# A hybrid decoder step on one core: the sample block's top-k laid over all 128 partitions

## The chip, the cores and the metric

The kernel runs on one core of a Trainium2 chip. The metric is the device time of one execution in microseconds (us); three executions of the kernel before took 1877.14, 1884.6 and 1884.9 us, median 1884.6.

## What is computed

One layer for 576 tokens: 512 of a prompt and 64 of a sample (8 sequences of 8 new tokens with a cache of 2048 positions). Attention with 12 heads over three dilated windows and a short convolution are joined by an output projection; then comes a channel mixer (PEER) that picks, for every token and each of 8 heads, 16 of 16384 single-neuron experts. That mixer is where the change lies:

```python
q = (xc @ wq).reshape(-1, 8, 2, 128)                 # 16 column blocks: head, half
s = einsum('nhpc,hpkc->nhpk', q, sub_keys)           # 128 scores per head and half
sv, si = top_k(s, 16)                                # first top-k: 16 of 128
cand = sv[:, :, 0, :, None] + sv[:, :, 1, None, :]   # pairs; ids likewise from si
top, pos = top_k(cand, 16)                           # second top-k: 16 experts per head
g = softmax(top)
act = gelu(einsum('nd,nhkd->nhk', x, u[eid]))
out = einsum('nhk,nhkd->nd', g * act, v[eid])
```

## The kernel before

The 576 tokens lie in five blocks: 0 to 3 are the prompt's, 128 tokens each; block 4 is the sample, 64 tokens. Tokens lie on partitions. All float32 products are made as three products of a high and a low part: `split` (L102) lets ScalarE copy the high part (L103) and VectorE subtract it (L104).

Instructions are written in program order, and a scheduler then sets the order on each engine; it may pull an instruction of a later stage forward to where it expects the engine to be free. Within an engine the order is fixed after that. Each engine, and each DMA queue (SP's here), takes its instructions one after the other.

The stages, with the names that the trace shows:

- Projections and attention (to about 480 us), with block 0 taken through the mixer's top-k early.
- `group(GB, ...)` for blocks 1 to 4: output projection (to about 560 us), then the loop over 16 column blocks of `wq` (L690), one for each head and half. Each step loads and splits the weights (`wraw`, `whi`, `wlo`), makes the queries of all 448 tokens (`mm`), copies them (`qc`, L698), multiplies them by the sub-keys (L703), copies the scores (`scs`, L705 for the three full blocks and L707 for the sample's 64 rows) and calls `topk1` for each block.
- `topk1` (L490) is five VectorE instructions on one head and half: eight largest (L495), replaced by a very small number (L496, writes `tkw`), the next eight (L497), and the places of both (L498, L499). Results go to `sv` and `si`.
- `topk2` (L501) takes a block's 8 heads: candidate pairs and their ids (`cand`, `cid`, L515), five instructions per head on 50 candidates (L523 to L527), the softmax (`gt` or `gatg`), and then the chosen ids by comparing, multiplying and summing over wide int16 tiles (`oh`, L547, L549, L554).
- The three prompt blocks 1 to 3 don't gather experts: all 16384 are computed (dense), and the chosen gates are placed in a table G. `gbuild` (L812) makes that table from `topk2`'s result, with one-hot tiles on VectorE (`oj`, L844; `oi`, L848), a scaled copy on ScalarE (`oi`, L852), products (`pG`) and a copy out (`stg`, L860) that is stored to DRAM (`Gd`).
- `ustep` (L773) is one of 128 steps of the dense mixer's first half: load 128 experts (`ur`), split (`uh`, `ul`), 24 products of 384 columns (`pu`), gelu (`a`, L782), and for the first 68 steps a store (`Ad`). These 68 are written between the pieces of `gbuild`.
- Then a loop over 128 steps of the second half (L935): the other 60 usteps come with it, each step loads `vr`, splits it, multiplies the gelu outputs by the table (`w`, L898) and makes 18 products of 512 columns (`y`, L909 to L913).
- Blocks 0 and 4 gather their experts instead: POOL fetches a row of `u` or `v` for each of 128 partitions (`row`, L469), VectorE takes the dot product (`jk`, L477) or adds it in (`accg`, L487). 128 rows of each table for block 0, 64 for the sample, which has 128 choices per token but lies on 64 partitions: its second half of choices is moved to partitions 64 to 127 (L572 to L574) and both halves are added at the end. This work is pushed in small units between the other stages (`pump`).

Of the kernel before, what the change touches and what calls it, by code (L numbers as in the profile page):

```python
# [19 lines left out]
P = 128  # L20
# [47 lines left out]
def body(tc, I, O):  # L68
# [421 lines left out]
    def topk1(st, cc, b, n, src):  # L490
        hd_, p_ = divmod(cc, 2)
# [9 lines left out]
    def topk2(st, b, n, ef, gat):  # L501
        sv, si = st[b]
        sf = tk.tile([P, 8, 2, 16], F32, name="sf")
        nc.vector.tensor_copy(sf[:n], si[:n])
        nc.vector.tensor_scalar(sf[:n, :, 0, :], sf[:n, :, 0, :], 128.0, None, op0=OP.mult)
        cand = tk.tile([P, 8, NCAND], F32, name="cand")
        cid = tk.tile([P, NCAND, 8], I16, name="cid")
        for src, dst in ((sv, cand), (sf, cid.rearrange("p w h -> p h w"))):
            o = 0
            for (a0, a1_, nb_) in PAIRS:  # L510
                na = a1_ - a0
                out = dst[:n, :, o:o + na * nb_].rearrange("p h (a b) -> p h a b", b=nb_)
                i0 = src[:n, :, 0, a0:a1_].unsqueeze(3).to_broadcast([n, 8, na, nb_])
                i1 = src[:n, :, 1, 0:nb_].unsqueeze(2).to_broadcast([n, 8, na, nb_])
# [3 lines left out]
        tv = tk.tile([P, 8, 16], F32, name="tv")  # L518
        tp = tk.tile([P, 8, 16], U32, name="tp")
        wc = tk.tile([P, NCAND], F32, name="wc", bufs=2)  # L520
        for hd_ in range(8):
            src = cand[:n, hd_, :]
            nc.vector.max(tv[:n, hd_, 0:8], src)  # L523
            nc.vector.match_replace(wc[:n], tv[:n, hd_, 0:8], src, -3.0e38)
            nc.vector.max(tv[:n, hd_, 8:16], wc[:n])
            nc.vector.max_index(tp[:n, hd_, 0:8], tv[:n, hd_, 0:8], src)
            nc.vector.max_index(tp[:n, hd_, 8:16], tv[:n, hd_, 8:16], wc[:n])  # L527
            if hd_ % 2:
                yield 1.2
        tf = tk.tile([P, 16, 8], I16, name="tf")  # L530
        nc.vector.tensor_copy(tf[:n], tp[:n].rearrange("p h k -> p k h"))
        te = tk.tile([P, 8, 16], F32, name="te")
        nc.vector.tensor_tensor(te[:n], tv[:n], tv[:n, :, 0:1].to_broadcast([n, 8, 16]), op=OP.subtract)
        nc.scalar.activation(te[:n], te[:n], AF.Exp)
        dn = tk.tile([P, 8], F32, name="dn")
        nc.vector.tensor_reduce(dn[:n], te[:n], axis=mybir.AxisListType.X, op=OP.add)
        nc.vector.reciprocal(dn[:n], dn[:n])
        nc.vector.tensor_tensor(gat[:n].rearrange("p (h k) -> p h k", h=8), te[:n],
                                dn[:n].unsqueeze(2).to_broadcast([n, 8, 16]), op=OP.mult)
        yield 1.0  # L540
        efv = ef[:n].rearrange("p (h k) -> p h k", h=8)
        for k0 in (0, 8):
            w = FIRST[k0 + 7] + 1
            oh = tk.tile([P, NCAND, 8, 8], I16, name="oh")
            ohf = oh.rearrange("p w k h -> p w (k h)")
            sel = tf[:n, k0:k0 + 8, :].rearrange("p k h -> p (k h)").unsqueeze(1).to_broadcast([n, w, 64])
            nc.vector.tensor_tensor(ohf[:n, :w], iotaw[:n, :w], sel, op=OP.is_equal)  # L547
            yield 1.7
            nc.vector.tensor_tensor(oh[:n, :w], oh[:n, :w], cid[:n, :w].unsqueeze(2).to_broadcast([n, w, 8, 8]),  # L549
                                    op=OP.mult)  # L550
            yield 1.7
            while w > 1:
                m = w - w // 2
                nc.vector.tensor_tensor(ohf[:n, :w - m], ohf[:n, :w - m], ohf[:n, m:w], op=OP.add)  # L554
                w = m
            nc.vector.tensor_copy(efv[:, :, k0:k0 + 8], oh[:n, 0].rearrange("p k h -> p h k"))
            yield 2.0

    def topk_gather(st, b, n, k):
        ef = tk.tile([P, SLOTS], F32, name="ef", bufs=2)  # L560
        if n == P:
            yield from topk2(st, b, n, ef, gatg[k])
            nc.vector.tensor_copy(idxg[k], ef)
            return
        gt = tk.tile([P, SLOTS], F32, name="gt", bufs=2)
        ei = tk.tile([P, SLOTS], I32, name="ei")
        yield from topk2(st, b, n, ef, gt)
        hs = SLOTS // 2
        nc.vector.tensor_copy(ei[:n], ef[:n])
        nc.vector.tensor_copy(idxg[k][:n, :hs], ef[:n, :hs])  # L570
        nc.vector.tensor_copy(gatg[k][:n, :hs], gt[:n, :hs])
        nc.sync.dma_start(idxg[k][n:2 * n, :hs], ei[:n, hs:])  # L572
        nc.sync.dma_start(gatg[k][n:2 * n, :hs], gt[:n, hs:])
        nc.sync.dma_start(x2g[k][n:2 * n, :], x2g[k][:n, :])  # L574

    def group(grp, st, chp, clp, mm, psc, x2dst, lname, pre2=None):
# [113 lines left out]
        for cc in range(16):  # L690
# [9 lines left out]
            sc = gp.tile([P, 4, P], F32, name="scs", bufs=2)  # L700
# [3 lines left out]
            full = [bi for bi, b in enumerate(grp) if BLKS[b][1] == P]  # L704
            nc.scalar.activation(sc[:, :len(full), :], p2[:, :len(full), :], AF.Copy)  # L705
# [329 lines left out]
```

## Time and profile before

| | |
|---|---|
| three executions | 1877.14, 1884.6, 1884.9 us |
| profiled execution, first to last instruction | 1882.2 us (no other time of it is given) |
| PE busy | 1738.2 us, 92% |
| VectorE (DVE) busy | 1430.9 us, 76%, 3064 instructions |
| ScalarE (ACT) busy | 881.6 us, 47% |
| POOL busy | 579.0 us, 31% |
| DMA | 533.75 MB, mean 284 GB/s |
| mean granted TensorE clock | 0.955 of full |

Busy shares are means over stages with different limits; the rows further down take the stages apart. Matmuls overlap each other, so a stretch in which PE is busy throughout may still hold fewer matmuls than another of the same length.

### The profile page before, as it was taken

Reading aid. Unit: us, or ns where it says so; the run is one execution under the profiler, and the core shown is the slowest. Engines: PE = TensorE matmul, PEld = TensorE weight load, DVE = VectorE, ACT = ScalarE, POOL = GpSimd, SP = SyncE. Lnnn points to the kernel's source line nnn. Section 1 sums busy time; section 2 is a strip of 40 time slices with the busy share of each in tenths; the row PEclk is TensorE's granted clock in tenths of the full one; section 3 lists DMA queues with packets and bytes.
Section 4 is the critical chain, followed back from the end, with each engine's and each line's share of the span. In section 5 each row is a group of like instructions: output and inputs, shape, how many; then the busy total and the mean of one; then the engine's idle time right before and its main releaser. Section 6 shows DMA issues by size and latency. Waiting matters only on the chain. (4 is left out here: it accounts for less than half of the span.)

```text
span 1882.2 us, 29066 instructions
## 1 busy us (share of the span) xinstructions
PE 1738.2 (92%) x10391; PEld 1467.3 (78%) x10391; DVE 1430.9 (76%) x3064; ACT 881.6 (47%) x1615; POOL 579.0 (31%) x483
## 2 busy tenths in 40 slices
PE   7999899997679999988988999999999999999997
PEld 5778655654558998987978889999999997777776
DVE  5433235766888999998788578888888778888888
ACT  4222366645323333479999933333333333333334
POOL 1010201014554214311212234544444444333330
PEclk9999979978788999999999999999999999999999
DMA  4257569858898448867777699999999999999996
GB/s 143 100 181 288 208 245 337 316 185 291 302 320 302 154 143 312 277 216 267 266 261 250 253 365 330 353 335 348 331 336 341 320 361 334 363 344 367 340 349 210
DMA packets 199077, 533.75 MB, mean 284 GB/s; under 512 B 17586, under 2 KB 82660, under 8 KB 197268
## 3 DMA queue, kind: packets, MB, share of 16 engines
q1 hardware_dynamic: 133364, 294.22, 44.0%
q0 software_dynamic: 65568, 237.69, 35.5%
q8 instruction: 81, 1.33, 0.3%
q14 instruction: 64, 0.52, 0.1%
HBM read 485.65 MB, written 45.63 MB: 282 GB/s over the span
## 5 line engine op out<-in xcount | busy, mean ns | idle before, releaser
L469 POOL DMA_INDIRECT row<-in_u,idxg x192 | 257.9, 1343 | 457.6 <-DVE avg L477 231.4
L469 POOL DMA_INDIRECT row<-in_v,idxg x192 | 264.5, 1377 | 421.6 <-DVE accg L487 345.3
L107 PE MATMUL pu<-x2h,uh 128*128 128x384 f32 x1024 | 350.9, 343 | 21.4 <-ACT a L782 11.1
L109 PE MATMUL pu<-x2h,ul 128*128 128x384 f32 x1024 | 352.0, 344 | 7.5 <-DVE ul L104 7.3
L108 PE MATMUL pu<-x2l,uh 128*128 128x384 f32 x1024 | 348.8, 341 | 0.0
L103 ACT ACTIVATE vh<-vr 128x1024 fp32r<-128x1024 f32 x128 | 135.8, 1061 | 290.4 <-PE y L913 251.4
L477 DVE CUSTOM_DVE_ANT_0 jk<-row,x2g 128x1024 bf16<-128x1024 f32 x192 | 233.8, 1218 | 28.0 <-DMA row<-in_u,idxg 26.8
L487 DVE SCALAR_TENSOR_TENSOR accg<-row,avg,accg 128x1024 f32<-128x1024 f32 x190 | 243.2, 1280 | 7.7 <-DMA row<-in_v,idxg 6.7
L909 PE MATMUL y<-vh,wh 128*128 128x512 f32 x768 | 224.7, 395 | 15.5 <-ACT wh L103 15.5
L911 PE MATMUL y<-vl,wh 128*128 128x512 f32 x768 | 234.2, 393 | 0.0
L107 PEld LDWEIGHTS pu<-x2h,uh 128*128 128x128 f32 x1024 | 196.5, 192 | 27.1 <-ACT a L782 12.2
L104 DVE TENSOR_TENSOR vl<-vr,vh 128x1024 fp32r<-128x1024 f32 x128 | 156.6, 1224 | 77.9 <-ACT vh L103 74.9
L913 PE MATMUL y<-vh,wl 128*128 128x512 f32 x768 | 215.6, 390 | 0.0
L109 PEld LDWEIGHTS pu<-x2h,ul 128*128 128x128 f32 x1024 | 196.4, 192 | 12.4 <-DVE ul L104 10.1
L103 ACT ACTIVATE uh<-ur 128x1024 fp32r<-128x1024 f32 x128 | 136.0, 1064 | 145.1 <-PE pu L108 74.1
L108 PEld LDWEIGHTS pu<-x2l,uh 128*128 128x128 f32 x1024 | 196.3, 192 | 1.7
L104 DVE TENSOR_TENSOR ul<-ur,uh 128x1024 fp32r<-128x1024 f32 x128 | 156.2, 1220 | 35.9 <-ACT uh L103 34.2
L909 PEld LDWEIGHTS y<-vh,wh 128*128 128x128 f32 x768 | 143.9, 189 | 46.5 <-ACT wh L103 19.5
L911 PEld LDWEIGHTS y<-vl,wh 128*128 128x128 f32 x768 | 145.1, 189 | 30.4
L913 PEld LDWEIGHTS y<-vh,wl 128*128 128x128 f32 x768 | 144.0, 188 | 30.1
L104 DVE TENSOR_TENSOR wlo<-wraw,whi 128x1024 fp32r<-128x1024 f32 (+1 forms) x96 | 91.0, 952 | 67.5 <-ACT whi L103 67.1
L103 ACT ACTIVATE whi<-wraw 128x1024 fp32r<-128x1024 f32 (+1 forms) x96 | 79.8, 840 | 124.3 <-PE mm L109 53.7
(281 smaller groups left out, 2936.4 us busy)
## 6 DMA issues: line engine op xcount, KB each, us to landing
ur<-in_ut SPq DMA_DIRECT2D x128, 512.0 KB
vr<-in_v SPq DMA_DIRECT2D x128, 512.0 KB
kt<-in_ck SPq DMA_DIRECT2D x60, 512.0 KB
vt<-in_cv POOLq DMA_DIRECT2D x60, 512.0 KB
Gd<-stg SPq DMA_DIRECT2D x12, 2048.0 KB
gt<-Gd SPq DMA_DIRECT2D x32, 768.0 KB
wraw<-in_w_in SPq DMA_DIRECT2D x24, 512.0 KB
Ad<-a SPq DMA_DIRECT2D x62, 192.0 KB
```

The lines of the kernel that those rows point to most:

```text
L103: nc.scalar.activation(hi, src, AF.Copy)
L104: nc.vector.tensor_tensor(lo, src, hi.bitcast(F32), op=OP.subtract)
L107: nc.tensor.matmul(out, ah, bh, start=first, stop=False)
L108: nc.tensor.matmul(out, ah, bl, start=False, stop=False)
L109: nc.tensor.matmul(out, al, bh, start=False, stop=last)
L469: nc.gpsimd.indirect_dma_start(out=r, out_offset=None, in_=I[src], in_offset=bass.IndirectOffsetOnAxis(ap=idx[:, s:s + 1], axis=0))
L477: nc.vector.tensor_tensor_reduce(jk, r, x2, 1.0, 0.0, OP.mult, OP.add, av[:, s:s + 1]))
L487: nc.vector.scalar_tensor_tensor(acc, r, av[:, s:s + 1], acc, op0=OP.mult, op1=OP.add))
L909: nc.tensor.matmul(accs[b][k], wh[:, sl], vh[:, k * 512:k * 512 + 512], start=first, stop=False)
L911: nc.tensor.matmul(accs[b][k], wh[:, sl], vl[:, k * 512:k * 512 + 512], start=False, stop=False)
L913: nc.tensor.matmul(accs[b][k], wl[:, sl], vh[:, k * 512:k * 512 + 512], start=False, stop=last)
```

## The change

The sample's scores for heads 4 to 7 are written to partitions 64 to 127, those of heads 0 to 3 stay on partitions 0 to 63. The score product of the 64 sample tokens goes to rows 0 or 64 of its bank, and the copy to a tile `sc4` keeps them there. One `topk1` on 128 partitions then serves two heads, so the column blocks of `wq` are taken in the order 0, 8, 1, 9, ... and the sample's `topk1` is called at every second one. `topk2` for the sample runs with 4 heads on 128 partitions, and gates and ids come out where the gather wants them. The copies and the two DMAs that moved them there are gone; the DMA that copies the sample's normed rows (`x2g`) to partitions 64 to 127 stays.

The diff, cut to its core (of `topk2` a few lines stand for all: `n` and 8 become `P` and `H`):

```diff
     def topk1(st, cc, b, n, src):
-        hd_, p_ = divmod(cc, 2)
+        hd_, p_ = divmod(cc % 8 if b == 4 else cc, 2)
...
-    def topk2(st, b, n, ef, gat):
+    def topk2(st, b, H, ef, gat):
         sv, si = st[b]
+        K = 8 * H
-        cand = tk.tile([P, 8, NCAND], F32, name="cand")
+        cand = tk.tile([P, 8, NCAND], F32, name="cand")[:, :H]
...
-        for hd_ in range(8):
-            src = cand[:n, hd_, :]
+        for hd_ in range(H):
+            src = cand[:, hd_, :]
...
-            nc.vector.tensor_tensor(ohf[:n, :w], iotaw[:n, :w], sel, op=OP.is_equal)
+            nc.vector.tensor_tensor(ohf[:, :w], iotaw[:, :w, :K], sel, op=OP.is_equal)
...
-        gt = tk.tile([P, SLOTS], F32, name="gt", bufs=2)
-        ei = tk.tile([P, SLOTS], I32, name="ei")
-        yield from topk2(st, b, n, ef, gt)
-        hs = SLOTS // 2
-        nc.vector.tensor_copy(ei[:n], ef[:n])
-        nc.vector.tensor_copy(idxg[k][:n, :hs], ef[:n, :hs])
-        nc.vector.tensor_copy(gatg[k][:n, :hs], gt[:n, :hs])
-        nc.sync.dma_start(idxg[k][n:2 * n, :hs], ei[:n, hs:])
-        nc.sync.dma_start(gatg[k][n:2 * n, :hs], gt[:n, hs:])
-        nc.sync.dma_start(x2g[k][n:2 * n, :], x2g[k][:n, :])
+        if H < 8:
+            nc.sync.dma_start(x2g[k][64:128, :], x2g[k][:64, :])
+        yield from topk2(st, b, H, ef, gatg[k][:, :16 * H])
+        nc.vector.tensor_copy(idxg[k][:, :16 * H], ef)
...
-        for cc in range(16):
+        for cc in [c for lo in range(8) for c in (lo, lo + 8)]:
...
+            up_ = cc // 8 * 64
             for bi, b in enumerate(grp):
                 t0, n = BLKS[b]
-                nc.tensor.matmul(p2[:n, bi, :], qc[:, t0 - g0:t0 - g0 + n], skT[:, cc, :], start=True, stop=True)
+                r0 = up_ if n < P else 0
+                nc.tensor.matmul(p2[r0:r0 + n, bi, :], qc[:, t0 - g0:t0 - g0 + n], skT[:, cc, :], start=True, stop=True)
...
+            if not up_:
+                sc4 = gp.tile([P, P], F32, name="sc4", bufs=2)
+            nc.scalar.activation(sc4[up_:up_ + 64, :], p2[up_:up_ + 64, nb - 1, :], AF.Copy)
+            for bi, b in enumerate(grp[:-1]):
+                topk1(st, cc, b, P, sc[:, bi, :])
+            if up_:
+                topk1(st, cc, 4, P, sc4)
...
-    drain(topk_gather(st, 4, 64, 1))
+    drain(topk_gather(st, 4, 4, 1))
```

What this does to the order, at three places. The first is VectorE in the `wq` loop; `sv_5199` and `si_5200` are the sample's results, the other numbers are those of blocks 1 to 3. Before, one step's turn of the four blocks:

```order
L495 MAX sv_5195<-scs 128x8
L495 MAX sv_5197<-scs 128x8
L496 MATCH_REPLACE tkw<-sv_5195,scs 128x128
L495 MAX sv_5199<-scs 64x8
...
L498 MAX_INDEX si_5200<-sv_5199,scs 64x8
...
L499 MAX_INDEX si_5200<-sv_5199,tkw 64x8
```

Now the sample reads its own tile (`sc_6294`) and stands there in every second step only:

```order
L495 MAX sv_5195<-scs 128x8
L495 MAX sv_5197<-scs 128x8
L496 MATCH_REPLACE tkw<-sv_5193,scs 128x128
L495 MAX sv_5199<-sc_6294 128x8
...
L498 MAX_INDEX si_5200<-sv_5199,sc_6294 128x8
L497 MAX sv_5195<-tkw 128x8
L499 MAX_INDEX si_5194<-sv_5193,tkw 128x8
```

In all, VectorE issues 62 rows fewer: 40 of `topk1`, 20 of the heads in `topk2`, 2 copies. The second place is VectorE where the table G is done (last `oj`) and the second half's loop begins (first `w`). Before:

```order
L844 TENSOR_TENSOR oj<-iotaj,JT 128x1024
L104 TENSOR_TENSOR ul<-ur,uh 128x1024 x6
L104 TENSOR_TENSOR vl<-vr,vh 128x1024
L898 TENSOR_TENSOR w<-a,gt 128x384 x2
L104 TENSOR_TENSOR wl<-w,wh 128x384
```

Now (lines here are those of the changed kernel: `oj` is L838, `w` L892):

```order
L838 TENSOR_TENSOR oj<-iotaj,JT 128x1024
L104 TENSOR_TENSOR ul<-ur,uh 128x1024
L487 SCALAR_TENSOR_TENSOR accg_2404<-row,avg_2407,accg_2404 128x1024
...
L104 TENSOR_TENSOR ul<-ur,uh 128x1024
L104 TENSOR_TENSOR vl<-vr,vh 128x1024 x2
L892 TENSOR_TENSOR w<-a,gt 128x384
L104 TENSOR_TENSOR wl<-w,wh 128x384
```

Six `ul` stand between the two in both, but they are other steps: counted from the start, before has 29 `ul` ahead of the first `oj`, 68 ahead of the last and 74 ahead of the first `w`; now it is 26, 63 and 69. Ahead of the 20th `w` it is 89 and 90. From the 60th `w` on both have the same counts of every kind (128 `ul`, 176 `jk`, 128 `accg`). The third place is SP's DMA queue near the end of the table; before:

```order
L863 DMA Gd<-stg 128x4096
L767 DMA ur<-in_ut 128x1024 x2
L572 DMA idxg_5203<-ei 64x64
L767 DMA ur<-in_ut 128x1024 x2
L863 DMA Gd<-stg 128x4096
```

Now:

```order
L761 DMA ur<-in_ut 128x1024 x2
L857 DMA Gd<-stg 128x4096
L761 DMA ur<-in_ut 128x1024 x2
L761 DMA vr<-in_v 128x1024
L885 DMA gt<-Gd 128x12x128
```

The two DMAs of `idxg` and `gatg` no longer stand among the loads of `ur`; the one of `x2g` stands at the same place as before, ahead of the `wq` loop.

## Rows read from the trace of the kernel before

**Rows 1.** The page's busy shares, then PE's 40 slices of the span.

```profile
PE 1738.2 (92%) x10391; PEld 1467.3 (78%) x10391; DVE 1430.9 (76%) x3064; ACT 881.6 (47%) x1615; POOL 579.0 (31%) x483
PE   7999899997679999988988999999999999999997
```

**Rows 2.** Windows by stage: stretch, length, busy time by engine, clock, DMA.

```profile
587.00:801.00 214.00, 207.58 (x1138) 196.10 (x1138) 207.02 (x848) 74.12 (x117) 67.98 (x48) 0.99 0.68 226
801.00:1068.00 267.00, 232.33 (x1668) 219.70 (x1667) 226.46 (x483) 252.29 (x552) 58.22 (x34) 0.94 0.72 254
811.00:1072.00 261.00, 229.60 (x1672) 217.46 (x1673) 218.13 (x459) 252.52 (x558) 56.74 (x33) 0.94 0.73 259
1300.00:1569.00 269.00, 269.00 (x1357) 244.06 (x1355) 219.46 (x270) 93.72 (x127) 123.43 (x96) 1.00 0.95 337
```

**Rows 3.** Windows of 20 us: PE at full pace, then three holes.

```profile
740.00:760.00 20.00, 20.00 (x117) 20.00 (x116) 19.37 (x67) 10.19 (x13) 5.63 (x5) 1.00 0.86 291
720.00:740.00 20.00, 15.48 (x79) 14.84 (x78) 18.21 (x73) 5.60 (x7) 11.33 (x7) 0.91 0.85 280
880.00:900.00 20.00, 14.06 (x97) 13.25 (x96) 18.73 (x55) 18.59 (x40) 5.31 (x3) 0.83 0.66 232
980.00:1000.00 20.00, 15.29 (x96) 14.08 (x95) 14.33 (x24) 19.94 (x42) 1.28 (x1) 0.74 0.62 231
```

**Rows 4.** Waits from 697 to 800 us: who for whom, us in total, times, longest.

```profile
ACT uh L103 <- DMA ur<-in_ut: 30.3, 10, 4.9
ACT uh L103 <- PE pu L108: 24.4, 9, 7.4
PEld pu L109 <- DVE ul L104: 8.0, 7, 3.5
```

**Rows 5.** Waits from 800 to 1043 us.

```profile
DVE oi L848 <- ACT oi L852: 14.3, 9, 3.1
PE pu L107 <- ACT a L782: 11.1, 5, 2.8
ACT uh L103 <- PE pu L108: 9.2, 3, 5.9
ACT stg L860 <- PE pG L858: 4.3, 3, 1.9
```

**Rows 6.** Timeline of VectorE: start, us, instruction; one turn of four blocks.

```profile
658.37 0.27 DVE L495 MAX8 sv<-scs 128x8 f32<-128x128 f32 x1
...
663.04 1.20 DVE L477 CUSTOM_DVE_ANT_0 jk<-row,x2g 128x1024 bf16<-128x1024 f32 x1
```

**Rows 7.** Groups by shape: line, engine, operation, count | busy us, mean ns | idle before.

```profile
L498 DVE FIND_INDEX8 si<-sv,scs 128x8 uint32<-128x128 f32 x48 | 13.1, 280 | 0.0
L498 DVE FIND_INDEX8 si<-sv,scs 64x8 uint32<-64x128 f32 x16 | 4.5, 280 | 0.0
L547 DVE TENSOR_TENSOR oh<-iotaw,tf 64x3200 int16<-64x3200 int16 x1 | 1.8, 1819 | 0.0
L547 DVE TENSOR_TENSOR oh<-iotaw,tf 64x2624 int16<-64x2624 int16 x1 | 1.5, 1508 | 0.0
L554 DVE TENSOR_TENSOR oh<-oh 64x1600 int16<-64x1600 int16 x1 | 1.0, 978 | 0.0
L554 DVE TENSOR_TENSOR oh<-oh 64x64 int16<-64x64 int16 x3 | 0.5, 182 | 0.0
L103 ACT ACTIVATE uh<-ur 128x1024 fp32r<-128x1024 f32 x128 | 136.0, 1064 | 145.1 <-PE pu L108 74.1 <-DMA ur<-in_ut 45.7 <-issue 16.2
L782 ACT ACTIVATE a<-pu 128x384 f32<-128x384 f32 x128 | 61.7, 482 | 19.8 <-PE pu L109 18.9 <-ACT a L782 0.9
```

**Rows 8.** SP's own waits from 800 to 1100 us.

```profile
SPq L767 <- DVE idxg L570: 3.8, 1, 3.8
SPq L767 <- DVE gt L538: 3.0, 1, 3.0
```

**Rows 9.** Line 898: count, ns shortest/median/longest, first and last start.

```profile
L898 DVE TENSOR_TENSOR w<-a,gt x66: 545/552/559, 1093.7 to 1857.3; 128x384 f32<-128x384 f32 x66
```

More of the change, by code (lines that the diff above doesn't have):

```diff
@@ L511, in topk2 @@
                 na = a1_ - a0
[L512 to L514 removed]
+                out = dst[:, :, o:o + na * nb_].rearrange("p h (a b) -> p h a b", b=nb_)
+                i0 = src[:, :, 0, a0:a1_].unsqueeze(3).to_broadcast([P, H, na, nb_])
+                i1 = src[:, :, 1, 0:nb_].unsqueeze(2).to_broadcast([P, H, na, nb_])
                 nc.vector.tensor_tensor(out, i0, i1, op=OP.add)
@@ L517, in topk2 @@
             yield 1.2
-        tv = tk.tile([P, 8, 16], F32, name="tv")
-        tp = tk.tile([P, 8, 16], U32, name="tp")
+        tv = tk.tile([P, 8, 16], F32, name="tv")[:, :H]
+        tp = tk.tile([P, 8, 16], U32, name="tp")[:, :H]
         wc = tk.tile([P, NCAND], F32, name="wc", bufs=2)
-        for hd_ in range(8):
-            src = cand[:n, hd_, :]
[L523 to L527, printed above, removed]
+        for hd_ in range(H):
+            src = cand[:, hd_, :]
+            nc.vector.max(tv[:, hd_, 0:8], src)
+            nc.vector.match_replace(wc, tv[:, hd_, 0:8], src, -3.0e38)
+            nc.vector.max(tv[:, hd_, 8:16], wc)
+            nc.vector.max_index(tp[:, hd_, 0:8], tv[:, hd_, 0:8], src)
+            nc.vector.max_index(tp[:, hd_, 8:16], tv[:, hd_, 8:16], wc)
@@ L528, in topk2 @@
             if hd_ % 2:
                 yield 1.2
[L530 to L536, printed above, removed]
@@ L537, in topk2 @@
-        nc.vector.reciprocal(dn[:n], dn[:n])
-        nc.vector.tensor_tensor(gat[:n].rearrange("p (h k) -> p h k", h=8), te[:n],
-                                dn[:n].unsqueeze(2).to_broadcast([n, 8, 16]), op=OP.mult)
+        tf = tk.tile([P, 16 * 8], I16, name="tf")[:, :16 * H].rearrange("p (k h) -> p k h", h=H)
+        nc.vector.tensor_copy(tf, tp.rearrange("p h k -> p k h"))
+        te = tk.tile([P, 8, 16], F32, name="te")[:, :H]
+        nc.vector.tensor_tensor(te, tv, tv[:, :, 0:1].to_broadcast([P, H, 16]), op=OP.subtract)
@@ L540, in topk2 @@
+        nc.scalar.activation(te, te, AF.Exp)
+        dn = tk.tile([P, 8], F32, name="dn")[:, :H]
+        nc.vector.tensor_reduce(dn, te, axis=mybir.AxisListType.X, op=OP.add)
+        nc.vector.reciprocal(dn, dn)
+        nc.vector.tensor_tensor(gat.rearrange("p (h k) -> p h k", h=H), te,
+                                dn.unsqueeze(2).to_broadcast([P, H, 16]), op=OP.mult)
         yield 1.0
-        efv = ef[:n].rearrange("p (h k) -> p h k", h=8)
+        efv = ef.rearrange("p (h k) -> p h k", h=H)
@@ L542, in topk2 @@
         for k0 in (0, 8):
             w = FIRST[k0 + 7] + 1
-            oh = tk.tile([P, NCAND, 8, 8], I16, name="oh")
-            ohf = oh.rearrange("p w k h -> p w (k h)")
-            sel = tf[:n, k0:k0 + 8, :].rearrange("p k h -> p (k h)").unsqueeze(1).to_broadcast([n, w, 64])
-            nc.vector.tensor_tensor(ohf[:n, :w], iotaw[:n, :w], sel, op=OP.is_equal)
+            ohf = tk.tile([P, NCAND * 64], I16, name="oh")[:, :NCAND * K].rearrange("p (w c) -> p w c", c=K)
+            oh = ohf.rearrange("p w (k h) -> p w k h", h=H)
@@ L714, in mkst @@
     def mkst(pl, grp):
-        return {b: (pl.tile([P, 8, 2, 16], F32, name=f"sv{b}"), pl.tile([P, 8, 2, 16], U32, name=f"si{b}"))
-                for b in grp}
+        return {b: tuple(pl.tile([P, 4 if b == 4 else 8, 2, 16], dt, name=f"{nm}{b}")
+                         for nm, dt in (("sv", F32), ("si", U32))) for b in grp}
     st0 = mkst(keep2, GA)
@@ L814, in gbuild @@
         gt = tk.tile([P, SLOTS], F32, name="gt", bufs=2)
-        yield from topk2(st, b, P, ef, gt)
+        yield from topk2(st, b, 8, ef, gt)
         ei = tk.tile([P, SLOTS], I32, name="ei")
```

35 lines of the change are left out of this document (13 added, 22 removed).

## The prediction, on record before the changed kernel ran

> **What bounds the kernel now.** First the page: PE is busy 92% of the span, VectorE 76%, and of its 40 slices most from the 14th on show a full PE [rows 1]. A share of the whole span says little here, so I cut the part that the change touches into stretches. Stretch A, 587 to 801 us, holds the `wq` loop with its top-k and then the second top-k of the first dense block. In it VectorE is busy 207.0 of 214.0 us and PE 207.6 [rows 2]. Stretch B, 801 to 1068 us, builds the table G; there ScalarE is busy 252.3 of 267 us, VectorE 226.5, PE 232.3 [rows 2]. Behind it the second half's loop keeps PE busy without a gap, 269.00 of 269 us from 1300 to 1569 [rows 2].
>
> How much of a busy PE is work shows best in the pace. At full clock, from 740 to 760 us, 117 matmuls fill 20.00 us [rows 3], 0.171 us each; a `ustep` of 24 takes 4.1 us. Where PE really loses time are holes: 720 to 740 us, 15.5 us busy at clock 0.91; 880 to 900, 14.1 at 0.83; 980 to 1000, 15.3 at 0.74 [rows 3]. In the first of them PE waits for `ul` from a VectorE that has top-k standing ahead of it, 8.0 us in 7 waits, while ScalarE waits 30.3 us for loads of `ur` and 24.4 us for PE to hand back buffers [rows 4]. In B the waits end at ScalarE: VectorE waits 14.3 us for the scaled one-hot tiles, PE 11.1 us for gelu; ScalarE itself waits only for PE, 9.2 and 4.3 us, and for VectorE nowhere among the longest [rows 5].
>
> From this follows how to count. Usteps are the filler that the scheduler pulls forward to keep PE busy in A and B. If A or B gets shorter with as many usteps in it, the end comes earlier by as much. If usteps fall out of A or B, each is done later, where PE has no free time, and costs 4.1 us.
>
> **The change part by part.**
>
> First top-k. The sample's 16 turns become 8, each on 128 partitions. An instruction on 64 partitions takes as long as on 128: 280 and 280 ns for the same form [rows 7]. One turn of four blocks runs from 658.37 to 663.04 us [rows 6], 4.67 us, so 1.17 us per block. Eight turns fewer are 9.3 us of VectorE, all in A, where its queue is nearly full.
>
> Second top-k of the sample, all in B and spread over it. Four heads fewer: five instructions each, taken like a turn of the first top-k, 1.17 us at most, 4.7 us together. The compare and the multiply over wide tiles, 1.82 and 1.51 us [rows 7], each twice, 6.7 us, work on half the elements and save 3.3 at most. Twelve sums from 0.98 down to 0.18 us [rows 7] save some 2. The small ones hardly get shorter: those on 64 elements still take 0.18. Together between 7 and 10 us; I take 9.4.
>
> What left the end of the sample's top-k. Two small copies on VectorE, and two DMAs in SP's queue. Behind them stood loads of `ur`, which waited 3.8 and 3.0 us because SP first waited for the ids and the gates [rows 8]. Both waits lie in B, while ScalarE is busy 19.94 of 20 us (from 980, [rows 3]) and wouldn't have split an earlier `ur`: I cost this at nothing, and 6.8 us at most if ScalarE's queue gets thinner. Who needs the ids of the sample is its gather; its dot products stand behind the 40th `w` in both orders, so an earlier list of ids is worth nothing.
>
> What stays the same. As many score products, as many copies by ScalarE, as many loads of `wq` of the same size in another order. The DMA of `x2g` keeps its place in SP's queue. The sample's first top-k waits for two steps of the loop instead of one; nothing queued behind it on VectorE needs it before the sample's `topk2`, late in B.
>
> The order of the filler. By the fences above, 26 instead of 29 usteps are split before B's one-hot tiles begin, 63 instead of 68 before they end. So A has 3 usteps fewer, B 2 fewer (37 for 39), and 5 come later.
>
> A: PE has 3 x 4.1 = 12.3 us less to do, VectorE 9.3 for the top-k and, with three `ul` and three dot products of about 1.2 us each that move out, 7.3 more: 16.6, of which some 2.5 comes back as the next block's heads move in. Both queues were nearly full, so A shrinks by what the slower of them loses: from 12.3 to 16.6, taken 14.
>
> B: ScalarE's own work falls by two usteps, 2 x (1.06 + 0.48) = 3.1 us [rows 7]. Of the 261 us between its first and last scaled tile it was busy 252.5 [rows 2]; the 8.5 us of idle time could close at most. VectorE got about 13 us lighter there (9.4, two `ul`, and a few gather units that are placed elsewhere), but it was not what ScalarE waited for [rows 5], so I give it half of these 8.5: B shrinks by 3.1 to 11.6, taken 7.
>
> After B: 5 usteps x 4.1 = 20.5 us more. From the 20th `w` on the count of usteps is one ahead of before's, from the 60th all counts agree, so nothing else is added, and the tail runs the same list.
>
> Sum: -14 - 7 + 20.5 = -0.5 us; at the ends -12.3 - 3.1 + 20.5 = +5.1 and -16.6 - 11.6 + 20.5 = -7.7. Made against the profiled span of 1882.2 us that is 1881.7. The three executions have their median 2.4 us above that span, one below it; I add the sum to the median: 1884. So nearly 19 us of VectorE work go, and I expect none of it in the time: it becomes idle time of VectorE, because the scheduler answers a shorter top-k with less filler, and the filler was paid in PE's time all along.
>
> **The rivals.**
>
> VectorE sets both stretches. For it: 207.0 of 214 us in A, a PE that waits for `ul` in the hole at 720 [rows 3, 4], and two holes at 880 and 980, where the sample's second top-k stood in the queue with the next block's. Then A loses 16.6, B in proportion to VectorE's load 267 x 13 / 226.5 = 15, and the hole of 4.5 us at 720 closes: -16.6 - 15 - 4.5 + 20.5 = -16, 1869. Against it: B's rows name ScalarE [rows 5].
>
> The change doesn't shorten the later part of A at all, because there loads set the pace. From 697 to 800 us ScalarE waits 30.3 us for `ur` [rows 4] with the DMA at 0.85 [rows 3]. Loads and gathered rows of that part are the same 17 usteps and 17 rows in both orders, so only the top-k's 9.3 us go from A. If B keeps its 267 us too, since the same one-hot tiles and gate copies pass ScalarE, the five displaced usteps decide: -9.3 + 20.5 = +11, 1896. It decides as soon as A and B together shrink by less than 20.5 us, and can be told from no change when they shrink by less than 11. For it: the scheduler moves usteps by its own idea of durations, not by what the chip waits for. Against it: `ur` waits are ScalarE's, which has 74 of 214 us to do in A [rows 2].
>
> PE sets A by itself. Its 207.6 us of 214 leave 6.4 us to win, and what A then loses is only its displaced usteps, 12.3; B likewise loses two, 8.2, which makes 0.0 with the 20.5. This can't be told from my forecast by the time, only by VectorE's idle time. The Trainium skill ("Trainium Kernel Development and Optimization", Performance Expectations) calls matmul busy time a bad measure, since matmuls are pipelined, and weight loads' busy share a good one. By weight loads A is 196.1 of 214 us full [rows 2], which would leave 18 us to win and side with the first rival; that the pace in the hole at 720 is 79 matmuls for 117 agrees with there being something to win.
>
> **How the numbers follow.** Within 0.5% of the median, that is 1875 to 1894 us, a measurement of this kernel can hardly tell a change from none, its three executions being 0.4% apart. The forecast and the third rival, both within that, get 0.52 together. VectorE as the bound gets 0.27, and 0.03 more goes to a faster tail by other transfers' luck: faster 0.30. The loads as the bound get 0.18: slower 0.18. The likeliest case by itself spans 1877 to 1890, from the ends of the sum about the median. The range of 8 in 10 takes in the first rival's 1869 and most of the second's 1896: 1868 to 1895.
>
> **What would show it.** VectorE's busy time should fall by about 19 us, its instructions by 62 and their loads. The last score copy should come 9 to 14 us earlier. In a window from the first to the last scaled one-hot tile ScalarE should again be busy over 95%, with a length of 250 to 258 us; if that is under 248, VectorE was the bound. The first `w`, at 1093.7 us before [rows 9], should come near 1073, but the 20th when it came before, because five usteps lie between. If the 20th `w` is over 10 us early, my count of the filler is wrong; if the first `w` is less than 10 us early, the loads were the bound. From the 60th `w` on stretches should have the same length in both.

## The result, and the profile after

The changed kernel takes 1893.0 us in the median of six runs (1888.7 to 1897.0), the kernel before 1883.9 on the same chip: a ratio of 1.0052, with a 95% interval of 1.0032 to 1.0073. A second group of runs gave 1895.2 beside 1881.8, ratio 1.0068 [1.0042, 1.0094]. The forecast was 1884 and no change; it is 9 to 13 us slower. The profiled execution has a span of 1890.0 us.

First the page after: busy shares, then PE's 40 slices.

```profile
PE 1743.5 (92%) x10391; PEld 1468.8 (78%) x10391; DVE 1415.2 (75%) x2966; ACT 882.6 (47%) x1615; POOL 566.9 (30%) x483
PE   7999899987779998988888999999999999999997
```

Against [rows 1] VectorE lost 15.7 us of work and 98 records: the 62 instructions of the forecast, and 36 loads of match values that the trace counts by themselves. PE has as many matmuls, and more holes.

Now the windows by stage, which answer to [rows 2]: A (590 to 791), B (791 to 1050), and a stretch of the second half.

```profile
590.00:791.00 201.00, 194.46 (x1064) 183.47 (x1063) 193.53 (x775) 72.56 (x112) 52.47 (x45) 0.98 0.66 221
791.00:1050.00 259.00, 226.02 (x1617) 211.42 (x1617) 213.86 (x448) 247.10 (x546) 40.02 (x33) 0.94 0.72 254
1242.00:1562.00 320.00, 320.00 (x1617) 290.92 (x1616) 259.82 (x306) 112.97 (x153) 153.38 (x111) 1.00 0.93 332
```

A is 13 us shorter than before, with three usteps fewer in it, and B 8 us, with two fewer. PE and VectorE stay nearly full in A, ScalarE is still busy 247 of 259 us in B. Both stretches got shorter by about what was forecast; the time went elsewhere.

To find where, I counted PE's **loss** in each stretch: its length, less the sum of its matmuls at full pace (for each form of matmul the interval from one start to the next that the shortest tenth of them stay within). The matmuls of all kernels here come to 1521 to 1522 us, so the span is this sum and the losses. The table gives two profiles of each kernel, and a profile is one execution. Marks between the stretches, each by its start: the first top-k instruction of the `wq` loop, the first and the 48th (last) one-hot tile on VectorE, the 20th `w`, the last `ul`, and the last `w`.

| loss of PE, us | before, twice | changed, twice |
|---|---|---|
| start to the first top-k of the loop | 238.0, 235.5 | 241.0, 241.4 |
| A | 20.1, 19.9 | 19.9, 20.4 |
| B | 62.4, 62.3 | 63.1, 62.2 |
| last one-hot tile to 20th `w` | 3.7, 2.7 | 7.4, 10.7 |
| 20th `w` to last `ul` | 3.7, 3.7 | 3.3, 3.3 |
| 50 us behind the last `ul` | 5.0, 3.4 | 8.7, 8.9 |
| from there to the last `w` | 16.0, 14.1 | 12.2, 13.4 |
| end | 11.8, 11.8 | 12.9, 12.9 |

In A and B PE loses what it lost before: what they got shorter is the work of the five usteps that left them. The mean difference of 14 us is 4.5 ahead of the change, 5.9 right behind B, 4.6 where the usteps end, and -1.1 in the rest. The first of these places isn't the work of the new order: the kernel with 32 unused bytes, which comes further down, has before's order there on VectorE, ScalarE and both DMA queues, and lost 244.2 us.

The place behind B, in windows of 10 us counted from the last one-hot tile (1067.8 us before, 1050.0 after), before and then after (columns as in [rows 2]):

```profile
1068.00:1078.00 10.00, 10.00 (x78) 9.52 (x77) 4.12 (x4) 10.00 (x19) 0.00 (x0) 1.00 0.41 145
1078.00:1088.00 10.00, 10.00 (x60) 10.00 (x59) 2.45 (x2) 3.89 (x6) 0.00 (x0) 1.00 0.93 356
1088.00:1098.00 10.00, 8.75 (x47) 7.93 (x46) 6.56 (x9) 4.79 (x8) 1.01 (x1) 1.00 1.01 344
1098.00:1108.00 10.00, 10.00 (x50) 8.76 (x49) 10.00 (x12) 3.95 (x5) 4.95 (x4) 1.00 1.04 404
```

```profile
1050.00:1060.00 10.00, 8.02 (x66) 7.38 (x64) 4.35 (x5) 9.82 (x18) 0.94 (x1) 1.00 0.73 272
1060.00:1070.00 10.00, 10.00 (x61) 10.00 (x60) 4.86 (x5) 3.99 (x5) 0.97 (x2) 1.00 0.98 369
1070.00:1080.00 10.00, 10.00 (x59) 9.95 (x58) 4.78 (x4) 4.54 (x6) 2.58 (x2) 1.00 1.05 389
1080.00:1090.00 10.00, 7.70 (x38) 6.33 (x36) 7.04 (x7) 3.98 (x5) 2.88 (x2) 1.00 1.05 386
```

From the second window on the DMA engines are full in both, 0.93 to 1.05, and before loses 1.6 us of PE with that, all in its third. The changed kernel loses it in two windows: 2.5 us in the first (before 0.3) and 3.0 in the fourth (before 0.2). In the first, PE waits for a `uh` that ScalarE makes late, and ScalarE is busy 9.82 of 10 us, mostly with the end of G (who waits for whom, us in total, times, longest; before has no such wait in its first window):

```profile
PE pu L107 <- ACT uh L103: 1.3, 1, 1.3
```

The second profile loses 4.2, 1.7, 0.1 and 1.9 us in these four windows, with a granted clock of 0.84 and 0.82 in the first two, for 1.00 above.

In the fourth window PE waits 1.7 us for the high part of the first `w` and 0.8 us for an `ul` whose load came late: ScalarE stood 2.9 us for that `ur`. SP's queue shows why. The columns of this timeline are start, length and instruction:

```profile
1064.37 4.49 SPq L761 DMA_DIRECT2D ur<-in_ut  x2
1068.96 0.43 SPq L761 DMA_DIRECT2D vr<-in_v  x1
1070.57 0.38 SPq L885 DMA_DIRECT2D gt<-Gd  x1
1071.00 3.67 SPq L761 DMA_DIRECT2D vr<-in_v  x2
1074.71 0.50 SPq L885 DMA_DIRECT2D gt<-Gd  x1
1075.27 5.74 SPq L890 DMA_DIRECT2D ar<-Ad  x2
1081.11 1.11 SPq L761 DMA_DIRECT2D ur<-in_ut  x2
```

For 12 us, from 1068.9 to 1081.1, no `ur` is issued (before, the gaps there are 7 to 8 us), while a ustep takes 4.1 and two buffers hold loads ahead. The first `w`, answering to [rows 9], came 10 us earlier, not 20 (1086.8 and 1089.8 us in the second profiles, 3 us earlier):

```profile
L892 DVE TENSOR_TENSOR w<-a,gt x66: 546/551/559, 1083.5 to 1863.4; 128x384 f32<-128x384 f32 x66
```

### The profile page after: what moved, and what is told of

Same layout as the page of the kernel before. It is cut to its first block, busy times and chain, and to the rows that moved or that the text cites. A ratio compares the mean times of both kernels' runs of the same rounds, so it can differ in the third digit from the quotient of the medians.

```text
span 1890.0 us, 28888 instructions
## 1 busy us (share of the span) xinstructions
PE 1743.5 (92%) x10391; PEld 1468.8 (78%) x10391; DVE 1415.2 (75%) x2966; ACT 882.6 (47%) x1615; POOL 566.9 (30%) x483
## 5 line engine op out<-in xcount | busy, mean ns | idle before, releaser
L469 POOL DMA_INDIRECT row<-in_u,idxg x192 | 248.8, 1296 | 493.8 <-DVE avg L477 224.4
L107 PE MATMUL pu<-x2h,uh 128*128 128x384 f32 x1024 | 349.7, 342 | 19.9 <-ACT a L776 10.1
L905 PE MATMUL y<-vl,wh 128*128 128x512 f32 x768 | 229.7, 391 | 3.2 <-DVE vl L104 3.2
L907 PE MATMUL y<-vh,wl 128*128 128x512 f32 x768 | 220.8, 390 | 0.0
L103 ACT ACTIVATE wh<-w 128x384 fp32r<-128x384 f32 x128 | 66.4, 521 | 169.3 <-DVE w L892 126.0
```

Source lines behind the costliest of these rows:

```text
L103: nc.scalar.activation(hi, src, AF.Copy)
L107: nc.tensor.matmul(out, ah, bh, start=first, stop=False)
L469: nc.gpsimd.indirect_dma_start(out=r, out_offset=None, in_=I[src], in_offset=bass.IndirectOffsetOnAxis(ap=idx[:, s:s + 1], axis=0))
L905: nc.tensor.matmul(accs[b][k], wh[:, sl], vl[:, k * 512:k * 512 + 512], start=False, stop=False)
L907: nc.tensor.matmul(accs[b][k], wl[:, sl], vh[:, k * 512:k * 512 + 512], start=False, stop=last)
```

## The experiments

Seventeen runs. Theory from the first on: VectorE's work is worth little, the list of instructions that the scheduler makes decides. "List" is the order of the instructions on each engine; "loss behind B" is that of the fourth row of the table.

**The order of the columns alone.** The kernel before, with

```
-        for cc in range(16):
+        for cc in [c for lo in range(8) for c in (lo, lo + 8)]:
```

> The kernel before with one line changed: the wq columns are taken as 0, 8, 1, 9. VectorE has as many instructions as before, and only four of them change places in its list. Theory (the extra time of the change comes from its new list of instructions, in three places: about 3 us ahead of the top-k, 4 us between the last one-hot tile and the first w, 4 us where the usteps end): 1884 us, ratio to before within 0.998 to 1.002. Rival (the order itself costs, because each pair of wq loads lies apart, or the second head of a pair comes late): 1889 us or more, ratio 1.003 to 1.006, with the loss between 587 and 800 us.

1882.8 us, ratio 1.0001 [0.9978, 1.0024]; A 214.1, B 266.5 us long, losses within 1 us of before's in every stretch. The order costs nothing. The reverse, the changed kernel in natural order (`for cc in range(16)`, and eight tiles `sc4` that wait for their upper half):

> The changed kernel with the wq columns in their natural order, 0 to 15: the sample's scores of the first eight turns wait in eight tiles of their own until the last eight turns, in which all of the sample's first top-k stands. 66 usteps ahead of the last one-hot tile, as with the added 32 bytes. Theory (the list decides; the order of the columns is worth nothing): 1880 us, ratio 0.996 to 1.001. Rival (the new order is what makes the change cost, or what makes it work): under 0.996 or over 1.004.

1887.0 us, 1.0022 [1.0000, 1.0043]: neither. Its A and B lose 18.1 and 58.1 us, less than those of the kernel before; its profile, of the slowest of its twelve executions (1895.4 us), lost 249.6 us ahead of the loop's first top-k, which the edit doesn't explain and which I leave open.

**The sample's tiles as large as before.** The changed kernel, with

```
-        return {b: tuple(pl.tile([P, 4 if b == 4 else 8, 2, 16], dt, name=f"{nm}{b}")
+        return {b: tuple(pl.tile([P, 8, 2, 16], dt, name=f"{nm}{b}")
```

and `topk2` reading the first four heads.

> The changed kernel with one thing put back: the sample's tiles for the values and ids of its first top-k have eight heads again, half of them unused, so that the tiles behind them lie where they lay before. VectorE's work is that of the changed kernel. In the instructions' order 66 usteps are split ahead of the last one-hot tile, for 63 in the changed kernel and 68 before: three of the five displaced usteps come back. Theory (a displaced ustep costs 4.1 us behind B and saves as much in A and B; what makes the time is the new list's losses of PE): no simple relation to the count; 1884 to 1893 us, the first w some 10 us later than in the changed kernel. Rival (the displaced usteps cost because they leave A and B, whose PE then idles; the placement of tiles is what displaced them): three fifths of the loss go, 1887.5 us or less, with A and B no longer than in the changed kernel.

1878.7 us, 0.9975 [0.9953, 0.9996], 14 us faster than the changed kernel for 1 KB of unused memory per partition. A is as long as in the changed kernel, 200.9 us, so that the rival (no longer) is right for A; B is 265.5 us, 7 more, with three usteps more. The time is below the theory's range, and the whole loss went, not the rival's three fifths. Is it the tile? The changed kernel with one line more,

```
     st = mkst(x2p, GB)
+    x2p.tile([P, 8], F32, name="padx")
```

> The changed kernel with one tile of 32 bytes per partition added behind the sample's tiles, which nothing reads or writes. Every instruction is that of the changed kernel, but the scheduler's list comes out as another one: on all five engines, instruction for instruction, that of the kernel with eight heads in the sample's tiles (66 usteps split ahead of the last one-hot tile, for 63). Theory (the list, above all the number of usteps in B, makes the time): 1879 us as that kernel, ratio to before 0.995 to 1.000. Rival (the lower time of that kernel is luck of the runs, or comes from where its tiles lie on the chip): 1893 us as the changed kernel, ratio 1.004 to 1.007.

1880.3 us, 0.9991 [0.9974, 1.0009]. The two kernels have the same list; their ratios overlap, and both lie clear of the changed kernel's 1.0032 to 1.0094. So most of the loss goes with the list, and 32 bytes that nobody uses decide which list there is. Two paddings of different size give one list and about one time, which speaks against the places of the tiles in memory; the changed kernel's own list with its tiles elsewhere wasn't run. Beside the changed kernel's two profiles the two of this list lose 4.5 us less in B, 3.7 less behind it and 5.4 less in the 50 us behind the last `ul`, but 2.1 us more ahead of the top-k, and 3.0 more between those 50 us and the last `w`. The windows of the kernel with 32 bytes, A and B:

```profile
593.00:796.00 203.00, 196.48 (x1068) 184.90 (x1067) 193.99 (x779) 72.59 (x113) 52.35 (x45) 0.98 0.66 220
796.00:1062.00 266.00, 237.62 (x1685) 224.09 (x1684) 219.74 (x449) 250.09 (x549) 43.96 (x35) 0.94 0.71 256
```

In B 40 usteps for 37 stand in 7 us more by these windows, 266.4 us for 258.7 and 257.9 by the marks, since PE's loss in B is 58.5 us, for 62.2 and 63.1. That is the list, not the price of a ustep in B: within this list two usteps fewer make B 9.6 us shorter, as the next runs show.

**VectorE's work given back.** To the changed kernel

```
+            topk1(stx, cc, 4, P, sc[:, 0, :]) if not up_ else None
...
-        for hd_ in range(H):
+        for hd_ in [x % H for x in range(8)]:
```

> The changed kernel with the VectorE work given back: in the eight turns in which the sample has no top-k, one is run on scores of another block into a tile that nobody reads (1.17 us each), and in the sample's second top-k the five instructions of each of its four heads run twice (1.1 us each): 13 to 14 us of VectorE in all. The output stays as it is. Theory (VectorE's work is no bound; what it saves becomes idle time): no slower than the changed kernel by over 0.2%, 1884 to 1896 us. Rival (VectorE sets A and B, and the gain of its shorter top-k is in the time of the changed kernel, hidden by a larger loss elsewhere): 1893 + 12 = 1905 us or more.

1885.9 us, 1.0013 [0.9989, 1.0038]: with 14 us more for VectorE it is no slower than the changed kernel, rather faster; its list has 66 usteps ahead of the last one-hot tile too, and its B loses 56.9 us. So B loses 62 to 63 us in the kernel before and in the changed one, with VectorE's work and without it, and 57 to 58.5 in the kernels with 66 usteps, again with it and without (all with LAG 68): the loss in B goes with the list. The two parts of the work, each on the kernel with the 32 bytes:

> The kernel with the added 32 bytes, and the first top-k's VectorE work given back: in the eight turns without the sample's top-k one is run into a tile that nobody reads, 9.3 us, all in A. 28 usteps are split ahead of the first one-hot tile, for 26, and 66 ahead of the last one, for 66. The output stays as it is. Theory (PE sets A, each ustep 4.1 us; VectorE's work is worth little there): A 8 us longer for its two usteps, B 3 us shorter for having two fewer, 1882 to 1885 us. Rival (VectorE sets A): A longer by 8 and by up to 9 more, 1888 us or more.

1882.9 us, 1.0005 [0.9986, 1.0024].

> The kernel with the added 32 bytes, and the five instructions of each of the four heads of the sample's second top-k run twice: 4.5 to 5 us of VectorE given back, all in B. Usteps ahead of the first and the last one-hot tile stay 26 and 66. The output stays as it is. Theory (ScalarE sets B): B no longer by over 1 us, 1878 to 1881 us, ratio to before 0.995 to 1.000. Rival (VectorE sets B): B and the time 5 us longer, 1884 us or more.

1882.5 us, 1.0007 [0.9990, 1.0024]. First the window of A of the former, then that of B of the latter:

```profile
591.00:801.00 210.00, 203.90 (x1115) 192.59 (x1114) 205.21 (x849) 75.86 (x116) 51.86 (x47) 0.98 0.66 224
```

```profile
793.00:1060.00 267.00, 239.11 (x1698) 224.96 (x1697) 224.16 (x487) 251.70 (x553) 42.14 (x35) 0.94 0.72 260
```

A got 7 us longer and holds 47 matmuls more, two usteps of 4.1; PE's loss in it is 19.4 us, for 20.6 without the work. The B behind it has two usteps fewer and is 256.8 us long for 266.4, not the 3 us shorter that I expected. With the heads back B kept its length within 0.3 us, with as many usteps and a loss of 57.4 for 58.5: 4.4 us of VectorE in B (224.16 for 219.74) are worth nothing there. For A the test is less clean, since the work brought its usteps along, and no run has the one without the other. There it is a fit: PE's loss stays at 19 to 21 us in these kernels, the one before and the changed one, while VectorE's idle time in A goes from 9.0 us (of 203) to 4.8 (of 210). In whole times the two stand 2 to 3 us above the kernel without that work, inside the intervals; the heads' 1882.5 lies between its two forecasts.

**How many usteps behind B.** The changed kernel and those with the other list, with LAG 64 or 72, and LAG 72 before as a control:

> The changed kernel with LAG 64 for 68: four of the usteps that stood between the last one-hot tile and the first w are done in the second half's loop instead, and there are four stores and four loads fewer of what gelu leaves. Theory (4 us of the loss are the stretch of usteps alone ahead of the first w, where loads of ur, vr, gt and ar come together): the first w about 16 us earlier, and 1889 us, ratio to before 1.001 to 1.004. Rival (the loss is that of the work that was moved, wherever it stands): 1893 us as the changed kernel, ratio 1.004 to 1.007.

> The kernel with eight heads in the sample's tiles, and LAG 64 for 68: ahead of the first w stand 71 usteps for 72, ahead of the 20th 86 for 90, and four stores and four loads of what gelu leaves are gone. It may beat both kernels. Theory (the stretch of usteps alone behind B loses some PE time, and fewer stand in it): 1872 to 1878 us, ratio 0.992 to 0.997. Rival (LAG 64 helped the changed kernel only because it has too many usteps behind B; here it takes none away there): 1879 us, ratio 0.996 to 1.000.

> The changed kernel with LAG 72 for 68: its list is the same up to the last one-hot tile (63 usteps), and 12 usteps for 6 stand between it and the first w. PE's loss (elapsed time less the time of its matmuls at their full pace) between the last one-hot tile and the 20th w was 7.4 and 10.7 us in the changed kernel's two profiles, 3 to 4 before. Theory (the first loads for the second half land some 30 us after the last one-hot tile, whatever PE does, and it runs short of filler there): with twice the filler PE loses 3 us or less there; 1886 to 1889 us, ratio 1.001 to 1.004. Rival (each ustep behind B is slow by itself, since its loads stand among those of the second half): 10 us of loss or more, ratio 1.006 or more.

> The kernel with the added 32 bytes and LAG 72 for 68: the same list up to the last one-hot tile (66 usteps), 8 usteps for 6 between it and the first w. PE's loss from there to the 20th w was 5.4 us with 68. It may beat both kernels. Theory (short of filler): 3 us or less there, 1877 us, ratio 0.995 to 0.999. Rival (each ustep behind B is slow by itself): a loss of 6 us or more there, ratio 1.000 or more.

> The kernel before with LAG 72 for 68, as a control on LAG alone: 68 usteps ahead of the last one-hot tile, six between it and the first w, as with 68. Theory (six are enough there only because 68 usteps were done in time): the loss between the last one-hot tile and the 20th w stays at 3 to 4 us, ratio 0.998 to 1.002. Rival (LAG 72 is better or worse by itself, through its four more stores and loads): a ratio outside of that, and then those of the other two are to be read against it.

| kernel | usteps from last one-hot tile to first `w` | loss behind B, us | ratio to before |
|---|---|---|---|
| before, 68 | 6 | 3.7, 2.7 | 1 |
| changed, LAG 64 | 6 | 5.4 | 1.0033 [1.0014, 1.0052] |
| changed, 68 | 6 | 7.4, 10.7 | 1.0052, 1.0068 |
| changed, 72 | 12 | 17.3 | 1.0086 [1.0068, 1.0104] |
| 8 heads, 68 | 6 | 5.3 | 0.9975 |
| 8 heads, 64 | 5 | 13.8 | 1.0069 [1.0050, 1.0088] |
| 32 bytes, 68 | 6 | 5.4 | 0.9991 |
| 32 bytes, 72 | 8 | 16.1 | 1.0053 [1.0028, 1.0077] |
| before, 72 | 6 | 5.3 | 1.0049 [1.0030, 1.0068] |

LAG 64 didn't do what I expected of it: the changed kernel's first `w` came at 1084.4 us for 1083.5, not 16 us earlier, with as many usteps ahead of it; five left the stretch from there to the 20th `w`. Its time lies in the theory's range, but not for that reason, and its interval meets the changed kernel's. My theory for LAG 72, that the gap wants more filler, fell: the loss doubled. The waits of the kernel with 32 bytes and LAG 72, 1060 to 1110 us, say why (who waits for whom, us in total, times, longest):

```profile
ACT uh L103 <- DMA ur<-in_ut: 11.1, 4, 5.8
PE pu L107 <- ACT uh L103: 9.5, 3, 7.5
```

The usteps there are starved of their own loads. Too few isn't good either, and LAG 64 with eight heads missed by 20 us: there PE stands for the first `w`, whose `gt` waits for the last store of G (the store is issued at 1074.8 us, this `gt` at 1082.1). Waits from 1060 to 1100 us, then one window:

```profile
PE y L903 <- ACT wh L103: 8.4, 1, 8.4
```

```profile
1080.00:1090.00 10.00, 1.55 (x9) 1.23 (x8) 3.75 (x5) 2.94 (x5) 0.00 (x0) 0.80 1.02 359
```

The place is narrow on both sides, but the count doesn't set the loss by itself: with six it is 2.7 to 10.7 us. LAG 72 costs the kernel before 0.5% too, so of what it cost the others a part isn't theirs alone: in its profile 10.2 us were lost in the 50 us behind the last `ul`. That profile is of the shortest of its executions, 1885.4 us for a median of 1892.2, so it doesn't show all of it.

**The `gt` loads out of SP's queue.** `nc.sync.dma_start(gt, ...)` became `nc.scalar.dma_start(gt, ...)`, in both:

> The changed kernel with the loads of gt issued from ScalarE's queue instead of SP's; up to the last one-hot tile the list stays. Behind B, SP issues no ur for 12.2 us in the changed kernel (1068.9 to 1081.1), because three vr, two gt and two ar stand between. Theory (the place of these loads in SP's queue is what starves the usteps behind B): with both gt gone from there the gap falls to 9 us or less, PE's loss from the last one-hot tile to the 20th w to 5 us or less (7.4 and 10.7 in the changed kernel), and the time by 3 us or more, ratio 1.000 to 1.005. Rival (the 16 DMA engines are full there, whatever the order): the same loss, 7 us or more, ratio 1.004 to 1.009.

> The same edit in the kernel with the added 32 bytes. It may beat both kernels. Theory: a loss from the last one-hot tile to the 20th w of 3 to 4 us for 5.4, 1877 us, ratio 0.995 to 0.999. Rival (DMA full): 1880 us, ratio 0.998 to 1.002, or more where ScalarE's queue stands still for a gt that waits for the last store of G.

1903.5 us, 1.0122 [1.0096, 1.0148], and 1893.7, 1.0066 [1.0042, 1.0091]; losses behind B of 13.8 and 11.7 us. The gap between issues of `ur` fell to 9 us as expected, and the loss rose: the queue's order alone isn't it. In the changed kernel with this edit the DMA is as full, and ScalarE stands still with the loads that it now issues (window, then a wait from 1050 to 1100 us):

```profile
1080.00:1090.00 10.00, 9.36 (x45) 9.23 (x45) 5.41 (x5) 3.17 (x5) 1.68 (x1) 0.83 1.07 384
```

```profile
ACT uh L103 <- issue: 4.4, 1, 4.4
```

That the full DMA alone makes the loss isn't shown by this, since the edit brought a wait of its own; and the kernel before has it as full behind its own last one-hot tile, without the loss. The first time is above both forecasts, the second fits only the rival's "or more".

**A third buffer for `ar`.** Behind the last `ul`, `w` waits for loads of `ar`: 9.7 us over the run in the changed kernel, 6.0 with 32 bytes, 4.6 before. The kernel with 32 bytes, with `ARB = 3` for 2:

> The kernel with the added 32 bytes, and three buffers for the loads of what gelu left (ARB 3 for 2). Up to the first w its list is that of the kernel with two. w waited for these loads 6.0 us in that kernel, 4.6 before, 9.7 in the changed one. It may beat both kernels. Theory (the hole where the usteps end is w waiting for a late load): 3 to 5 us less than with two buffers, 1876 us, ratio 0.994 to 0.998, and w's wait for the loads under 2 us. Rival (PE is short there of v, not of w): no gain, ratio 0.998 to 1.002.

`w` waited no more, yet the time was 1887.2 us, 1.0022 [1.0004, 1.0041]: PE's loss was 6.9 us in that place, for 4.4, and 20.0 from there to the last `w`, for 16.5. In that list `w` was late but not what PE lacked; the profile is of the shortest of its executions, 1882.8 us. For the changed kernel, windows counted from about 9 us behind the last `ul` show where it is short:

```profile
1570.00:1590.00 20.00, 16.87 (x70) 13.52 (x68) 12.95 (x20) 6.07 (x9) 9.08 (x7) 0.91 0.93 317
1590.00:1610.00 20.00, 16.92 (x74) 13.44 (x72) 16.52 (x28) 6.54 (x9) 8.82 (x7) 1.00 0.94 343
```

In the same windows of the kernel before, 1563 to 1583 and 1583 to 1603, there are 70 matmuls at a clock of 0.91, as here, and then 90 at 1.00 for 74. The order there is not the same. From the 60th `w` on VectorE has 341 records in both, but from the 13th of them they stand in another order, and so do the loads in SP's queue (from the 60th `w` on, before and then after, `gt` left out):

```profile
1570.82 0.33 SPq L767 DMA_DIRECT2D vr<-in_v  x1
1571.76 3.40 SPq L896 DMA_DIRECT2D ar<-Ad  x2
1580.83 0.33 SPq L767 DMA_DIRECT2D vr<-in_v  x1
```

```profile
1578.10 0.33 SPq L761 DMA_DIRECT2D vr<-in_v  x1
1579.04 10.25 SPq L890 DMA_DIRECT2D ar<-Ad  x3
1591.25 0.33 SPq L761 DMA_DIRECT2D vr<-in_v  x1
```

A third `ar` stands ahead of the `vr`, which is issued 13 us behind the one before it, for 10; on VectorE a `w` stands ahead of the `vl` and waits 2.85 us for its `ar`. The kernel with 32 bytes keeps before's order there up to the 46th record. Most of the 4.6 us lie here; that the order makes them wasn't tried by itself.

**Both kernels again.** The kernel before, profiled once more, and the changed kernel:

> The kernel before once more, for a second profile: how far the lengths of its stretches repeat. Theory: the sample's first score again 3 us or more earlier than in the changed kernel; stretches within 1.5 us of the first profile's. Rival (such differences are chance of a profile): 2 us or more off in both directions.

> The changed kernel once more, for a second profile and for a comparison beside the other kernels of this group. Theory (its list costs 0.5 to 0.7% against the list that 32 bytes more give): ratio to before 1.003 to 1.007; the stretch from the first w to the start of the 100th 7 to 11 us longer than with the padded list's, and about 3 us more than before ahead of the sample's first score. Rival (its loss was luck of the first runs): 1.002 or less.

1876.8 us in the one run, and 1895.2 us, 1.0068. From the loop's first top-k on the stretches came again within 1 us in A and B, and the loss behind B within 3.3; ahead of it the kernel before lost 235.5 to 238.8 us in four profiles (the order alone and LAG 72 among them), the changed kernel 241.0 to 242.5 in five (with LAG 64, 72 and the `gt` edit, whose lists are the same up to there). But the kernels with 32 bytes or eight heads, which have before's order there, lost 242 to 247 us in seven profiles and 233.3 in the one with three `ar` buffers. So the order doesn't explain this difference.

## Why the prediction was wrong

**A and B: right, and by the third rival's numbers.** A is 12.6 us shorter (213.7 to 201.1), forecast 14; B 8.3 (267.0 to 258.7), forecast 7. That is 20.9 against the 20.5 of five usteps. 12.6 and 8.3 are almost 3 and 2 usteps of 4.1, and PE's losses are unchanged, as that rival had it. My split, VectorE for some of A and ScalarE's idle time for some of B, was right only in sum.

**VectorE isn't the bound.** The first rival fell: with its work given back PE loses no more in either stretch; in B that is shown with as many usteps, in A it is a fit. The Trainium skill ("Trainium Kernel Development and Optimization", Performance Expectations) prefers the weight loads' busy share to matmul busy time; by it A had 18 us to win. PE's loss in A was indeed about 20 us, so that as a measure of what is lost it agrees; but 9.3 us of VectorE's work more left it at 19.4.

**The loads.** The second rival had the right sign and time, 1896, by a mechanism that isn't there: A and B shrank by 21 us, not by 9.

**The step that failed** is the third line of the sum, "After B: 5 usteps x 4.1 = 20.5 us more", with "so nothing else is added, and the tail runs the same list". A ustep's price behind B was taken from PE's pace alone, and nothing was added for the order that it lands in. The runs show 5.9 us more of PE's loss right behind B, at the end of G and around the first `w`, and 4.6 us where the usteps end. There the tail doesn't run the same list: the counts agree from the 60th `w` on, as I had them, but the order doesn't. Another 4.5 us lie ahead of A, which I took as unchanged. Together 15.0, less 1.1 in the rest, where the span grew by 13.8 in the mean of two profiles each. That the first two go with the list is shown by the kernels with 32 bytes and with eight heads, which lose 5.4 and 5.3 us behind B and 4.4 and 2.4 where the usteps end. What of them is the late load, what ScalarE's queue and what the order of `ar` and `vr` wasn't taken apart, and the cause of the 4.5 us stays open.

**What I took as given** was that a shorter top-k makes the scheduler pull fewer usteps into A and B. In A it is so: with the turns given back 28 stand ahead of the first one-hot tile, for 26, and 29 before. But ahead of the last one the count is 66 in every kernel with the other list, whether VectorE has its work back or not, and three of the five displaced usteps left by the accident of a list. With 66 the two kernels of that list took 1880 and 1879 us, 0.1 and 0.25% below before; the other kernels with 66 and LAG 68 took 1882 to 1887 but for the `gt` edit.

**The marks.** "First `w` near 1073" missed by 10 us. Six usteps stand between the last one-hot tile and the first `w` in both kernels; the displaced ones stand behind it, 21 for 15 up to the 20th. But A began 3.1 us later, and that first stretch took 33.5 us for 25.9, of which 2.8 are PE's loss and the rest work that PE did there earlier. The text's own test, "less than 10 us early, the loads were the bound", stood at its edge, 10.2 (3.0 in the second profiles), while A and B had shrunk as forecast: it can't tell one from the other. The 20th `w` came 12.5 us late. VectorE lost 15.7 us, forecast 19; 2.4 of the missing 3.3 are the stop that is told of at the end. The last score copy came 9.3 us earlier and the window from the first to the last scaled one-hot tile was 253.8 us long with ScalarE 98.6% busy, both as forecast. From the 60th `w` to the end it took 312.1 and 313.5 us, for 311.5 and 308.0.

**What stays open**: why 32 bytes change the list, and what costs 4.5 us ahead of the top-k. A version that clearly beats before wasn't found; eight heads in the sample's tiles is the best, 0.25% with an interval that just leaves out 1.

## What to carry to other kernels

Where a scheduler fills PE's gaps, ask of work taken off an engine beside PE which holes in PE it makes or closes: sum PE's loss by stretch, before and after, with windows counted from the same event in both. Work that is displaced must be priced where it lands, in the order it lands in. Equal counts of instructions aren't an equal order. And a change of half a per cent should be run under a second list of instructions (a few bytes of unused memory can give one) before it is put down to the change itself.

## What the runs showed of the hardware

A stop of VectorE at the start of the first dense block's second top-k was not expected: its scaling of `sf` and its first replacement into `wc`, some 0.2 us in the other blocks, show 3.96 and 3.85 us in the changed kernel, 1.52 and 1.43 before. The row of `sf` in the changed kernel (durations shortest/median/longest in ns, first and last start):

```profile
L506 DVE TENSOR_SCALAR sf<-sf x5: 175/220/3955, 404.7 to 835.7; 128x128 f32<-128x128 f32 x4, 128x64 f32<-128x64 f32 x1
```

The stop came in both profiles of the changed kernel, and with 32 bytes and eight heads, and counts as busy in VectorE's share; what it is, no run shows.
